# A log-sum-exp kernel: 1.5 heads per tile through TensorE in full fp32, 20 load buffers, and a last tile in pieces

## The chip, the cores and the metric

The kernel runs on one core of a Trainium2 chip. The metric is device time in microseconds (us). "Time" is the median of several executions; "span" is the length of the one profiled execution, and is 1 to 2 us shorter. All times below are of fast-state runs, except where a sentence says otherwise.

Engine names in the profile: PE is TensorE, PEld its weight loads, DVE is VectorE, ACT is ScalarE, POOL is GpSimd, SP the engine that issues the loads.

## The reference

`x` is 8 x 2048 x 2048 in fp32 (134 MB), `bias` is 8 heads x 256. For each row and each head of 256 columns the kernel must return log(sum(exp(x + bias))), and each result is stored twice in a row.

```
x_heads = x.reshape(B, S, H, Dh).transpose(0, 2, 1, 3)      # H = 8, Dh = 256
x_heads = x_heads + bias[None, :, None, :]
x_tiled = np.repeat(x_heads, 2, axis=2)
mx = x_tiled.max(axis=-1, keepdims=True)
lse = mx.squeeze(-1) + np.log(np.exp(x_tiled - mx).sum(axis=-1))
```

## The kernel before

A tile is 128 rows x 2048 columns, 1 MiB; there are 128 of them. Seven of the eight heads go through VectorE: ScalarE takes exp of 1792 columns in one instruction, and VectorE multiplies each head with exp(bias) and sums it. The eighth head goes through TensorE: a first matmul writes the bias into PSUM (one row of ones as stationary operand, so a contraction over one row), a second adds x (identity as stationary operand). Both use the upper bf16 half of each number. ScalarE then takes exp of the result and sums it in the same pass.

```
XIN_BUFS = 8                                    # load buffers
pspool = ... tile_pool(name="pspool", bufs=3, space=PSUM)
...
for b in range(B):
    for sblk in range(nsblk):
        xt = xin.tile([P, D], mybir.dt.float32, name="xt")
        nc.sync.dma_start(out=xt, in_=x[b, s0 : s0 + P, :])
        ...                                     # x_hi, b_hi: views of the upper bf16 halves
        for h in range(n_ttr, H):               # n_ttr = 7: one head
            ps = pspool.tile([P, Dh], mybir.dt.float32, name="ps")
            nc.tensor.matmul(ps, lhsT=ones_bf[0:1, :], rhs=b_hi, start=True, stop=False)
            nc.tensor.matmul(ps, lhsT=ident_bf[:, :], rhs=x_hi, start=False, stop=True)
            nc.scalar.activation(out=ps, in_=ps, func=ACT.Exp,
                                 accum_out=R[:, b, h, sblk : sblk + 1])
        nc.scalar.activation(out=xt[:, 0 : n_ttr * Dh], in_=xt[:, 0 : n_ttr * Dh], func=ACT.Exp)
        for h in range(n_ttr):
            ...                                 # VectorE: multiply with exp(bias) and sum
    ...                                         # transpose of R, log, store, once per b
```

The softmax here doesn't subtract the row's maximum and nothing guards it: scores larger than these inputs give would overflow.

## Time and profile before

| | before |
|---|---|
| time | 347.4 us |
| VectorE busy | 92% |
| ScalarE busy | 79% |
| TensorE busy | 28% |
| DMA | 421 GB/s through the middle of the span |
| the last tile's load: 15 of 16 increments / the 16th | 327.8 us / 337.2 us |

The head of the page of the kernel before: first the busy time of each engine, then VectorE's and the DMA engines' rows of the table of 40 slices (each digit is a busy share in tenths), then what the DMA engines moved in each slice.

```profile
PE 95.0 (28%) x268; PEld 27.6 (8%) x268; DVE 316.6 (92%) x1793; ACT 272.4 (79%) x397; POOL 5.0 (1%) x15
...
DVE  0899989899898998999989989899899998999985
...
DMA  7999999999999999999999999999999999999700
GB/s 303 427 421 421 417 422 423 422 421 421 419 423 417 424 421 419 423 420 424 423 418 418 424 420 423 421 422 419 422 416 412 370 401 424 420 411 409 286 24 15
```

The loads fill nearly the whole span: 1 MiB at 421 GB/s takes 2.49 us (in the timeline a tile comes every 2.48), and VectorE needs 7 x 0.346 = 2.42 us per tile.

The view of waits of the kernel before says who waited for whom, for how many us in total, how often, and the longest.

```profile
PE ps L109 <- ACT ps L115: 207.5, 123, 2.1
ACT xt L123 <- DMA xt<-in_x_dram: 56.2, 105, 3.7
...
DVE junk L131 <- ACT xt L123: 15.4, 23, 1.0
```

The timeline of the kernel before, TensorE and ScalarE around one tile. The columns are start in us, duration, engine, line, operation and operands, and in brackets the idle time before it and what ended it.

```profile
156.20 0.37 ACT L115 ACTIVATE ps<-ps 128x256 f32<-128x256 f32 x1
...
156.50 0.18 ACT L115 ACTIVATION_READ_ACCUMULATOR ps<-ps 128x1 f32 x1
156.73 0.37 PE L109 MATMUL ps<-brow,ones_bf 1*128 1x256 bf16 x1 [1.81 <-ACT ps L115]
...
157.03 0.39 PE L112 MATMUL ps<-xt,ident_bf 128*128 128x256 bf16 x1
157.07 1.70 ACT L123 ACTIVATE xt<-xt 128x1792 f32<-128x1792 f32 x1 [0.39 <-DMA xt<-in_x_dram]
...
158.68 0.37 ACT L115 ACTIVATE ps<-ps 128x256 f32<-128x256 f32 x1
```

ScalarE ends a sum at 156.68, the bias matmul starts at 156.73, the x matmul at 157.03. Both are over by 157.42, while ScalarE is still in the large exp that its own wait for a load let start at 157.07. So the loop "ScalarE's sum, bias matmul, x matmul, ScalarE's next sum" takes about 1.2 us of work and fits inside the 2.48 us of a load.

### The profile page before, as it was taken

The numbers are of one execution on the slowest core, as the hardware profiler recorded it, in microseconds if no ns is written. First come the engines' busy times: TensorE is split into PE (matmuls) and PEld (weight loads), VectorE is DVE, ScalarE is ACT, GpSimd is POOL, SyncE is SP. The second block draws the span as 40 slices with busy tenths as digits, with TensorE's granted clock in tenths as the row PEclk, the third lists the DMA queues.
The fourth block names the chain that finished last, engine by engine and source line by source line (L and its number), as shares of the span: only waits on it lengthen the run. The fifth ranks groups of instructions, "written<-read, shape, count | busy, mean of one in ns | idle before, by whom it ended". The sixth has DMA issues, their size and how long they took to land. (4 is left out here: it accounts for less than half of the span.)

```text
span 345.5 us, 3541 instructions
## 1 busy us (share of the span) xinstructions
PE 95.0 (28%) x268; PEld 27.6 (8%) x268; DVE 316.6 (92%) x1793; ACT 272.4 (79%) x397; POOL 5.0 (1%) x15
## 2 busy tenths in 40 slices
PE   2423223223322323322332322232223232222220
PEld 0100000000000000000010000000000000000000
DVE  0899989899898998999989989899899998999985
ACT  4978878788787887878778878788777887878872
POOL 1000000000000000000000000000000000000000
DMA  7999999999999999999999999999999999999700
GB/s 303 427 421 421 417 422 423 422 421 421 419 423 417 424 421 419 423 420 424 423 418 418 424 420 423 421 422 419 422 416 412 370 401 424 420 411 409 286 24 15
DMA packets 18939, 135.50 MB, mean 392 GB/s; under 512 B 2177, under 2 KB 2305, under 8 KB 2529
## 3 DMA queue, kind: packets, MB, share of 16 engines
q1 hardware_dynamic: 18576, 134.36, 94.3%
q0 software_dynamic: 336, 0.92, 0.7%
q14 instruction: 23, 0.19, 0.1%
q8 instruction: 2, 0.03, 0.0%
q10 hardware_dynamic: 2, 0.01, 0.0%
HBM read 134.23 MB, written 1.05 MB: 392 GB/s over the span
## 5 line engine op out<-in xcount | busy, mean ns | idle before, releaser
L131 DVE CUSTOM_DVE_ANT_0 junk<-xt,w_rep 128x256 f32<-128x256 f32 x896 | 316.3, 422 | 24.0 <-ACT xt L123 15.4
L123 ACT ACTIVATE xt<-xt 128x1792 f32<-128x1792 f32 x128 | 217.2, 1698 | 62.7 <-DMA xt<-in_x_dram 56.2
L109 PE MATMUL ps<-brow,ones_bf 1*128 1x256 bf16 x128 | 46.9, 368 | 207.6 <-ACT ps L115 207.5
L131 DVE DVE_READ_ACCUMULATOR2_ANT R<- 128x1 f32 x896 | 74.8, 83 | 0.0
L112 PE MATMUL ps<-xt,ident_bf 128*128 128x256 bf16 x128 | 49.3, 385 | 21.4 <-DMA xt<-in_x_dram 21.3
L115 ACT ACTIVATE ps<-ps 128x256 f32<-128x256 f32 x128 | 47.2, 369 | 0.0
L112 PEld LDWEIGHTS <-ident_bf 128*128 128x128 bf16 x128 | 13.2, 104 | 245.2 <-issue 245.2
L115 ACT ACTIVATION_READ_ACCUMULATOR ps<-ps 128x1 f32 x128 | 23.5, 184 | 0.0
L109 PEld LDWEIGHTS <-ones_bf 1*128 1x128 bf16 x128 | 12.5, 98 | 45.6 <-issue 45.6
L152 ACT ACTIVATE res<-tps 128x256 f32<-128x256 f32 x8 | 3.1, 383 | 6.6 <-PE tps L143 6.6
L159 POOL DMA_DIRECT2D out_dram<-res x7 | 3.9, 562 | 295.9 <-ACT res L152 295.9
L143 PE MATMUL tps<-ident,R 128*128 128x128 f32 x8 | 3.6, 452 | 13.8 <-DVE R L131 13.8
L79 PE MATMUL psw<-brow,ones_bf 1*128 1x512 bf16 x4 | 2.4, 601 | 4.2 <-DMA brow<-in_bias_dram 2.4
L143 PEld LDWEIGHTS tps<-ident,R 128*128 128x128 f32 x8 | 1.4, 180 | 19.3 <-issue 15.8
L82 ACT ACTIVATE w_rep<-psw 128x512 f32<-128x512 f32 x4 | 2.3, 593 | 0.0
L50 ACT ACT_TABLE_LOAD x1 | 1.3, 1283 | 0.7 <-PEq L174 0.7
L63 DVE MEMSET ones_bf<- 1x128 bf16 x1 | 0.2, 165 | 0.8 <-PEq L174 0.8
L79 PEld LDWEIGHTS <-ones_bf 1*128 1x128 bf16 x4 | 0.5, 118 | 4.0 <-issue 3.0
masks.py:199 POOL TENSOR_SCALAR_AFFINE_SELECT ident<-ident 128x128 f32<-128x128 f32 x1 | 0.3, 285 | 0.0
masks.py:199 POOL TENSOR_SCALAR_AFFINE_SELECT ident_bf<-ident_bf 128x128 bf16<-128x128 bf16 x1 | 0.3, 285 | 0.0
masks.py:197 POOL MEMSET ident<- 128x128 f32 x1 | 0.2, 205 | 0.3 <-POOLq L174 0.3
masks.py:197 POOL MEMSET ident_bf<- 128x128 bf16 x1 | 0.2, 206 | 0.0
(4 smaller groups left out, 0.4 us busy)
## 6 DMA issues: line engine op xcount, KB each, us to landing
xt<-in_x_dram SPq DMA_DIRECT2D x128, 1024.0 KB, 16.4
out_dram<-res POOLq DMA_DIRECT2D x7, 128.0 KB, 5.8
out_dram<-res SPq DMA_DIRECT2D x1, 128.0 KB
brow<-in_bias_dram ACTq DMA_DIRECT2D x1, 8.0 KB
```

The lines of the kernel that those rows point to most:

```text
L50: nc.scalar.add_instruction(mybir.InstLoadActFuncSet(name=nc.get_next_instruction_name(), act_func_set_id=set_idx,))
L63: nc.vector.memset(ones_bf, 1.0)
L79: nc.tensor.matmul(psw, lhsT=ones_bf[0:1, :], rhs=b_hi_c, start=True, stop=True)
L82: nc.scalar.activation(out=w_rep[:, c * WCH : (c + 1) * WCH], in_=psw, func=ACT.Exp)
L109: nc.tensor.matmul(ps, lhsT=ones_bf[0:1, :], rhs=b_hi, start=True, stop=False)
L112: nc.tensor.matmul(ps, lhsT=ident_bf[:, :], rhs=x_hi, start=False, stop=True)
L115: nc.scalar.activation(out=ps, in_=ps, func=ACT.Exp, accum_out=R[:, b, h, sblk : sblk + 1],)
L123: nc.scalar.activation(out=xt[:, 0 : n_ttr * Dh], in_=xt[:, 0 : n_ttr * Dh], func=ACT.Exp,)
L131: nc.vector.tensor_tensor_reduce(out=junk, in0=xt[:, sl], in1=w_rep[:, sl], scale=1.0, scalar=0.0, op0=ALU.mult, op1=ALU.add, accum_out=R[ ...
L143: nc.tensor.transpose(out=ps, in_=R[:, b].rearrange("p h s -> p (h s)"), identity=ident)
L152: nc.scalar.activation(out=res, in_=ps_view, func=ACT.Ln)
L159: out_eng.dma_start(out=ov, in_=res.rearrange("p s e -> p (s e)"))
```

## The change

The intent: take work from VectorE (6.5 instead of 7 heads per tile), add the bias with full fp32 precision on the TensorE path, give the loads more buffers, and shorten the end. Odd tiles send 2 heads through TensorE, even tiles 1. The core of the diff, with cuts:

```
-N_TTR_HEADS = 7
-XIN_BUFS = 8
+NPE_MAX = 2
+XIN_BUFS = 20
...
-    pspool = ... bufs=3 ...
+    pbias = ... bufs=5 ...
...
+    def biased(xt, b, blk, npe):
+        ps = pbias.tile([P, CMAX], F32, name="ps")
+        n = npe * Dh
+        nc.tensor.matmul(
+            ps[:, 0:n], lhsT=ones, rhs=brow[:, 0:n], start=True, stop=False
+        )
+        nc.tensor.matmul(
+            ps[:, 0:n], lhsT=ident, rhs=xt[:, 0:n], start=False, stop=True
+        )
+        for h in range(npe):
             nc.scalar.activation(...)          # exp and sum of one head
...
+            npe = 1 + t % 2
...
+            cuts = [0, 512, 1024, 1536, 2048] if last else [0, D]
+            for i in range(len(cuts) - 1):
+                nc.sync.dma_start(
+                    out=xt[:, cuts[i] : cuts[i + 1]], in_=src[:, cuts[i] : cuts[i + 1]]
                 )
```

`ones`, `ident`, `brow` and `xt` are all read as fp32 now.

More of the change, by code (lines that the diff above doesn't have):

```diff
@@ L8 @@
 from concourse.masks import make_identity
-N_TTR_HEADS = 7
-XIN_BUFS = 8
+F32 = mybir.dt.float32
+ACT = mybir.ActivationFunctionType
+ALU = mybir.AluOpType
+NPE_MAX = 2
+XIN_BUFS = 20
 @with_exitstack
@@ L26 @@
     H, Dh = bias.shape
-    assert D == H * Dh
-    assert S % P == 0
-    nsblk = S // P
-    NCOL = H * nsblk
-    assert NCOL <= P
-    n_ttr = max(0, min(N_TTR_HEADS, H))
-    ACT = mybir.ActivationFunctionType
-    ALU = mybir.AluOpType
+    assert D == H * Dh and S % P == 0
+    NBLK = S // P
+    NR = H * NBLK
+    MM = 512
+    CMAX = NPE_MAX * Dh
     const = ctx.enter_context(tc.tile_pool(name="const", bufs=1))
-    rpool = ctx.enter_context(tc.tile_pool(name="rpool", bufs=1))
     xin = ctx.enter_context(tc.tile_pool(name="xin", bufs=XIN_BUFS))
     junkp = ctx.enter_context(tc.tile_pool(name="junkp", bufs=2))
-    pspool = ctx.enter_context(tc.tile_pool(name="pspool", bufs=3, space=bass.MemoryType.PSUM))
-    pspoolw = ctx.enter_context(tc.tile_pool(name="pspoolw", bufs=2, space=bass.MemoryType.PSUM))
-    tpsum = ctx.enter_context(tc.tile_pool(name="tpsum", bufs=2, space=bass.MemoryType.PSUM))
-    resp = ctx.enter_context(tc.tile_pool(name="resp", bufs=2))
+    pbias = ctx.enter_context(
+        tc.tile_pool(name="pbias", bufs=5, space=bass.MemoryType.PSUM)
+    )
+    tpsum = ctx.enter_context(
+        tc.tile_pool(name="tpsum", bufs=2, space=bass.MemoryType.PSUM)
+    )
+    resp = ctx.enter_context(tc.tile_pool(name="resp", bufs=2))
+    brow = const.tile([1, D], F32, name="brow")
+    w_rep = const.tile([P, D], F32, name="w_rep")
+    ident = const.tile([P, P], F32, name="ident")
+    ones = const.tile([1, P], F32, name="ones")
+    R = const.tile([P, B, H, NBLK], F32, name="R")
     with tc.high_priority():
-        act_sets = list(get_activation_tables(nc.m.arch).items())
-        for set_idx, (_set_name, funcs) in enumerate(act_sets):
+        for set_idx, (_name, funcs) in enumerate(
+            get_activation_tables(nc.m.arch).items()
+        ):
             if ACT.Exp in funcs and ACT.Ln in funcs:
@@ L56 @@
                 break
-        ident = const.tile([P, P], mybir.dt.float32, name="ident")
-        make_identity(nc, ident)
-        ident_bf = const.tile([P, P], mybir.dt.bfloat16, name="ident_bf")
-        make_identity(nc, ident_bf)
-        ones_bf = const.tile([1, P], mybir.dt.bfloat16, name="ones_bf")
-        nc.vector.memset(ones_bf, 1.0)
-        brow = const.tile([1, D], mybir.dt.float32, name="brow")
         nc.scalar.dma_start(
@@ L68 @@
         )
-        w_rep = const.tile([P, D], mybir.dt.float32, name="w_rep")
-        brb = brow.bitcast(mybir.dt.bfloat16)
-        WCH = 512
-        for c in range(D // WCH):
-            b_hi_c = bass.AP(
-                tensor=brb.tensor,
-                offset=brb.offset + 2 * c * WCH + 1,
-                ap=[[brb.ap[0][0], 1], [2, WCH]],
-            )
-            psw = pspoolw.tile([P, WCH], mybir.dt.float32, name="psw")
-            nc.tensor.matmul(
-                psw, lhsT=ones_bf[0:1, :], rhs=b_hi_c, start=True, stop=True
-            )
-            nc.scalar.activation(
-                out=w_rep[:, c * WCH : (c + 1) * WCH], in_=psw, func=ACT.Exp
-            )
@@ L86 @@
-    R = rpool.tile([P, B, H, nsblk], mybir.dt.float32, name="R")
-    for b in range(B):
-        for sblk in range(nsblk):
-            s0 = sblk * P
-            xt = xin.tile([P, D], mybir.dt.float32, name="xt")
-            nc.sync.dma_start(out=xt, in_=x[b, s0 : s0 + P, :])
-            if n_ttr < H:
-                xb = xt.bitcast(mybir.dt.bfloat16)
-                bb = brow.bitcast(mybir.dt.bfloat16)
-            for h in range(n_ttr, H):
-                x_hi = bass.AP(
-                    tensor=xb.tensor,
-                    offset=xb.offset + 2 * h * Dh + 1,
-                    ap=[xb.ap[0], [2, Dh]],
-                )
-                b_hi = bass.AP(
-                    tensor=bb.tensor,
-                    offset=bb.offset + 2 * h * Dh + 1,
-                    ap=[[bb.ap[0][0], 1], [2, Dh]],
-                )
-                ps = pspool.tile([P, Dh], mybir.dt.float32, name="ps")
-                nc.tensor.matmul(
-                    ps, lhsT=ones_bf[0:1, :], rhs=b_hi, start=True, stop=False
-                )
-                nc.tensor.matmul(
-                    ps, lhsT=ident_bf[:, :], rhs=x_hi, start=False, stop=True
-                )
-                nc.scalar.activation(
-                    out=ps,
-                    in_=ps,
-                    func=ACT.Exp,
-                    accum_out=R[:, b, h, sblk : sblk + 1],
-                )
-            if n_ttr > 0:
-                nc.scalar.activation(
-                    out=xt[:, 0 : n_ttr * Dh],
-                    in_=xt[:, 0 : n_ttr * Dh],
-                    func=ACT.Exp,
-                )
-                for h in range(n_ttr):
-                    sl = slice(h * Dh, (h + 1) * Dh)
-                    junk = junkp.tile([P, Dh], mybir.dt.float32, name="junk")
-                    nc.vector.tensor_tensor_reduce(
-                        out=junk,
-                        in0=xt[:, sl],
-                        in1=w_rep[:, sl],
-                        scale=1.0,
-                        scalar=0.0,
-                        op0=ALU.mult,
-                        op1=ALU.add,
-                        accum_out=R[:, b, h, sblk : sblk + 1],
-                    )
-        ps = tpsum.tile([NCOL, P], mybir.dt.float32, name="tps")
@@ new lines @@
+        nc.vector.memset(ones, 1.0)
+        make_identity(nc, ident)
+        for c in range(0, D, MM):
+            psw = pbias.tile([P, MM], F32, name="ps")
+            nc.tensor.matmul(
+                psw, lhsT=ones, rhs=brow[:, c : c + MM], start=True, stop=True
+            )
+            nc.scalar.activation(out=w_rep[:, c : c + MM], in_=psw, func=ACT.Exp)
+    def biased(xt, b, blk, npe):
[3 more added lines that the diff above has]
+            ps[:, 0:n], lhsT=ones, rhs=brow[:, 0:n], start=True, stop=False
+        )
+        nc.tensor.matmul(
+            ps[:, 0:n], lhsT=ident, rhs=xt[:, 0:n], start=False, stop=True
+        )
+        for h in range(npe):
+            nc.scalar.activation(
+                out=ps[:, h * Dh : (h + 1) * Dh],
+                in_=ps[:, h * Dh : (h + 1) * Dh],
+                func=ACT.Exp,
+                accum_out=R[:, b, h, blk : blk + 1],
+            )
@@ new lines, in weigh @@
+    def weigh(xt, b, blk, h):
+        c = h * Dh
+        junk = junkp.tile([P, Dh], F32, name="junk")
+        nc.vector.tensor_tensor_reduce(
+            out=junk,
+            in0=xt[:, c : c + Dh],
+            in1=w_rep[:, c : c + Dh],
+            scale=1.0,
+            scalar=0.0,
+            op0=ALU.mult,
+            op1=ALU.add,
+            accum_out=R[:, b, h, blk : blk + 1],
+        )
+    t = 0
+    for b in range(B):
+        for blk in range(NBLK):
+            xt = xin.tile([P, D], F32, name="xt")
+            src = x[b, blk * P : (blk + 1) * P, :]
+            npe = 1 + t % 2
+            t += 1
+            c0 = npe * Dh
+            last = b == B - 1 and blk == NBLK - 1
+            cuts = [0, 512, 1024, 1536, 2048] if last else [0, D]
+            for i in range(len(cuts) - 1):
+                nc.sync.dma_start(
+                    out=xt[:, cuts[i] : cuts[i + 1]], in_=src[:, cuts[i] : cuts[i + 1]]
+                )
+            for i in range(len(cuts) - 1):
+                a = max(cuts[i], c0)
+                e = cuts[i + 1]
+                if i == 0:
+                    biased(xt, b, blk, npe)
+                if a < e:
+                    nc.scalar.activation(
+                        out=xt[:, a:e], in_=xt[:, a:e], func=ACT.Exp
+                    )
+                    for h in range(a // Dh, e // Dh):
+                        weigh(xt, b, blk, h)
+        tps = tpsum.tile([NR, P], F32, name="tps")
@@ L143 @@
         nc.tensor.transpose(
-            out=ps, in_=R[:, b].rearrange("p h s -> p (h s)"), identity=ident
+            out=tps, in_=R[:, b].rearrange("p h n -> p (h n)"), identity=ident
         )
-        res = resp.tile([NCOL, P, 2], mybir.dt.float32, name="res")
-        ps_view = bass.AP(
-            tensor=ps.tensor,
-            offset=ps.offset,
-            ap=[ps.ap[0], [1, P], [0, 2]],
+        res = resp.tile([NR, P, 2], F32, name="res")
+        tv = bass.AP(
+            tensor=tps.tensor, offset=tps.offset, ap=[tps.ap[0], [1, P], [0, 2]]
@@ L151 @@
         )
-        nc.scalar.activation(out=res, in_=ps_view, func=ACT.Ln)
+        nc.scalar.activation(out=res, in_=tv, func=ACT.Ln)
         ov = bass.AP(
@@ L155 @@
             offset=out.offset + b * H * 2 * S,
-            ap=[[2 * P, NCOL], [1, 2 * P]],
+            ap=[[2 * P, NR], [1, 2 * P]],
         )
```

## The prediction

> **What bounds it now.** The loads, and in the end one DMA engine of 16. The table of slices shows the DMA engines at 90% or more and some 421 GB/s from slice 2 to 36. In the timeline a matmul on x starts every 2.48 us, and the exp's waits end on the tile's load. A tile is 1 MiB, 64 KB per engine: 26.4 GB/s each. VectorE is close below (7 heads x 0.346 = 2.42 us per tile), ScalarE further (2.09 us).
>
> About every 22 us a tile comes some 0.95 us late (gaps of 3.4 us at 44, 65, 89, 110, 154, 201, 246, 290, 334 us). Just before each, the trace has an 8 KB packet of the instruction queue. 8 KB are 128 instructions; VectorE's 1,930 make 15. The Trainium skill ("Runtime: NRT & Kernel Launch", Instruction fetch mechanics) says that a sequencer fetches instructions by its own DMA queue, mostly hidden; this trace says not hidden. A load needs 16 increments; of the last tile's, 15 came by 327.8 us and one at 337.2 us. So VectorE's fetches appear to delay always the same engine, which sets the time: 3.2 + 128 x 2.485 + 15 x 1.0 = 336 us. Then come exp 1.7, seven reductions to 341.5, transpose 0.45, log 0.39, store: span 345.5 us.
>
> **What the change does.**
> - VectorE: 896 to 832 reductions, 2.25 us per tile. That widens slack, and drops 128 instructions: one fetch fewer, about -1.0 us, the main gain.
> - ScalarE: every second tile an exp shorter by 0.21 us and one more summed exp (0.48 us): 2.22 us on average, off the path.
> - TensorE: two bf16 matmuls of 0.38 us become fp32 ones of 256 or 512 columns. The skill ("FP8 and Floating Point Precision", TensorE Precision Notes) gives fp32 four passes. From the trace (512 bf16 columns 0.60 us, 256 0.37) I estimate 0.9 and 1.8 us per matmul, 5.3 us per two tiles against 5.2 available: just full. I expect sustained work to make TensorE faster, so it keeps up. Its larger instruction stream presumably goes through another DMA engine.
> - 20 buffers: the late engine had 6 to 7 tiles outstanding throughout (16.4 us from issue to landing) and never starved; the others don't set the time. About 0.
> - Last tile in four pieces: before, 4.3 us from landing to the last reduction. Now VectorE must still do tile 126's 7 heads (ready 1.75 us after its landing, which is 2.48 us before the last), then 6 heads: about 3.9 us. ScalarE does its pieces behind fp32 matmuls. Gain 0.2 to 0.6 us; 2 KB rows cost 0.1 back.
>
> **Prediction.** 347.47 - 1.0 - 0.4 + 0.1 = 346.2 us; 8 in 10 between 344.3 and 349.0. Faster by over 2%: 0.05; within 2%: 0.87; slower by over 2%: 0.08.
>
> **Right if** after shows: slices still at 421 GB/s; the last load landing near 336 us, one increment 10 us or more after the others; 14 late tiles; VectorE some 84% busy and idle on waits; TensorE well under 100%; the last reduction 4 us after the last landing.
>
> **Wrong if** fp32 matmuls run slower than estimated and ScalarE waits for them in order (slower, perhaps much); if TensorE's fetches fall on VectorE's DMA engine (+5 us); if 20 buffers let the late engine catch up (to -10 us).

## More of the kernel before

The program is scheduled by a framework: an instruction may be placed earlier in its engine's order than it stands in the source, as far as its data and buffers allow.

L109 is the bias matmul, L115 is ScalarE's exp and sum of a TensorE head. In 123 of 128 tiles the bias matmul waits for ScalarE. Here this is harmless, because TensorE has little to do.

## The result, and the profile after

| | before | after |
|---|---|---|
| time | 347.4 us (347.3 to 347.7) | 530.96 us (530.81 to 531.17) |
| TensorE / VectorE / ScalarE busy | 28 / 92 / 79% | 79 / 56 / 54% |
| last load landed | 337.2 us | 454.4 us |
| last VectorE sum ended | 341.5 us | 525.4 us |

The ratio is 1.529 (95% interval 1.527 to 1.531). A ratio here is the mean time of one kernel's fast runs over that of the other's of the same rounds, so it is not quite the ratio of the medians in the table.

The same parts of the page, after:

```profile
PE 416.9 (79%) x528; PEld 133.0 (25%) x528; DVE 298.7 (56%) x1665; ACT 285.9 (54%) x527; POOL 4.6 (1%) x13
...
DVE  1755655655556556556565565565655655646556
...
DMA  8999999986676776767767667767667686200000
GB/s 349 420 421 423 422 421 422 420 362 240 252 274 240 275 262 245 296 240 243 277 256 266 259 231 303 246 240 289 237 269 259 239 305 240 79 12 0 0 1 10
```

For eight slices (106 us) the loads run as before, while the 20 buffers fill. Then they fall to 230 to 305 GB/s: they wait for buffers. The 20 buffers hid the trouble for a while and changed nothing of it. No engine is at 100%, which suggests that engines wait for each other.

The view of waits, after:

```profile
PEld ps L83 <- ACT ps L90: 231.8, 119, 2.6
ACT ps L90 <- PE ps L86: 222.6, 115, 5.5
DVE junk L100 <- ACT xt L133: 214.8, 120, 5.6
...
PE ps L83 <- ACT ps L90: 97.5, 117, 1.1
```

TensorE (the weight load of the bias matmul, L83) waits for ScalarE's sum (L90), and ScalarE's sum waits for the x matmul (L86). Each waits for the other, and VectorE waits behind them because ScalarE's large exp (L133) stands behind its sums. The rows count idle time of an engine: the weight loads are idle during TensorE's own matmuls too, so what TensorE lost to ScalarE is the last row, 97.5 us, and not the first. The timeline shows one turn for two tiles, TensorE and ScalarE only:

```profile
306.10 2.07 PE L83 MATMUL ps<-brow,ones 1*128 1x512 f32 x2 [0.57 <-ACT ps L90]
...
308.10 2.08 PE L86 MATMUL ps<-xt,ident 128*128 128x512 f32 x2
310.21 0.37 ACT L90 ACTIVATE ps<-ps 128x256 f32<-128x256 f32 x1 [2.79 <-PE ps L86]
310.49 0.20 ACT L90 ACTIVATION_READ_ACCUMULATOR ps<-ps 128x1 f32 x1
310.72 0.37 ACT L90 ACTIVATE ps<-ps 128x256 f32<-128x256 f32 x1
311.00 0.19 ACT L90 ACTIVATION_READ_ACCUMULATOR ps<-ps 128x1 f32 x1
...
311.25 1.22 PE L83 MATMUL ps<-brow,ones 1*128 1x256 f32 x2 [1.07 <-ACT ps L90]
...
312.39 1.22 PE L86 MATMUL ps<-xt,ident 128*128 128x256 f32 x2
313.65 0.37 ACT L90 ACTIVATE ps<-ps 128x256 f32<-128x256 f32 x1 [0.87 <-PE ps L86]
...
314.18 1.22 PE L83 MATMUL ps<-brow,ones 1*128 1x512 f32 x1 [0.56 <-ACT ps L90]
```

From 306.10 to 314.18 are 8.08 us for two tiles, where the loads would allow 4.96. TensorE's part is 2.00 + 2.11 + 1.14 + 1.26 = 6.51 us, ScalarE's 1.04 + 0.53 = 1.57, and nothing overlaps. 58 such turns, seven of them 0.5 us longer for a transpose, fill the span from 37 to 510 us.

Why does the bias matmul wait for ScalarE, with five PSUM buffers? The order of TensorE's matmuls, early in the trace, tells it. An fp32 matmul of the source is two instructions here, and a row merges neighbours of one line and shows the first one's shape: x8 is four bias matmuls, x4 two.

```profile
25.37 5.48 PE L83 MATMUL ps<-brow,ones 1*128 1x512 f32 x8
30.79 2.08 PE L86 MATMUL ps<-xt,ident 128*128 128x512 f32 x2
32.79 2.92 PE L83 MATMUL ps<-brow,ones 1*128 1x512 f32 x4
35.65 1.22 PE L86 MATMUL ps<-xt,ident 128*128 128x256 f32 x2
37.43 2.07 PE L83 MATMUL ps<-brow,ones 1*128 1x512 f32 x2 [0.56 <-ACT ps L90]
39.44 2.08 PE L86 MATMUL ps<-xt,ident 128*128 128x512 f32 x2
42.58 1.22 PE L83 MATMUL ps<-brow,ones 1*128 1x256 f32 x2 [1.07 <-ACT ps L90]
43.73 1.22 PE L86 MATMUL ps<-xt,ident 128*128 128x256 f32 x2
```

A bias matmul needs no load, only a PSUM buffer, so it was placed as early as a buffer could be had. With the tiles counted from 1, the bias matmuls of tiles 6 to 9 run before the x matmul of tile 6 (25.37 and 30.79 us), and those of tiles 10 and 11 before that of tile 7. From 37.43 us on the bias is four tiles ahead: that of tile 12 comes before the x matmul of tile 8. Four of the five buffers then hold finished bias rows (tiles 8 to 11); the fifth is that of tile 7, which ScalarE frees by summing tile 7. TensorE's matmuls run in this order, so the x matmul of tile 8 stands behind the bias of tile 12. Tile 8 thus can't start on TensorE before ScalarE has finished tile 7, and further buffers would be filled the same way (five and one were run, below). The kernel before has the same order, two tiles ahead with its three buffers; its loop was just short enough.

The groups by shape give the price of one matmul instruction (busy us, mean ns of one). An fp32 matmul of the source is two of them, each with its own weight load:

```profile
L83 PE MATMUL ps<-brow,ones 1*128 1x512 f32 x128 | 132.3, 1135 | 35.4 <-ACT ps L90 35.4
L86 PE MATMUL ps<-xt,ident 128*128 128x512 f32 x128 | 131.6, 1132 | 0.0
...
L86 PE MATMUL ps<-xt,ident 128*128 128x256 f32 x128 | 77.5, 709 | 0.0
L83 PE MATMUL ps<-brow,ones 1*128 1x256 f32 x128 | 77.2, 705 | 62.1 <-ACT ps L90 62.1
```

In the timeline an fp32 matmul occupies TensorE for 2.00 us with 512 columns and 1.14 with 256. The difference, 0.86 us per 256 columns, is four times the 0.22 us that 256 columns cost in bf16 in the kernel before (0.60 us with 512 columns less 0.38 with 256). That agrees with the four passes of the Trainium skill ("FP8 and Floating Point Precision", TensorE Precision Notes).

### The profile page after: what moved, and what is told of

The parts are those of the page before. It is cut to its first block, busy times and chain, and to the rows that moved or that the text cites. A ratio compares the mean times of both kernels' runs of the same rounds, so it can differ in the third digit from the quotient of the medians.

```text
span 529.2 us, 3971 instructions
## 1 busy us (share of the span) xinstructions
PE 416.9 (79%) x528; PEld 133.0 (25%) x528; DVE 298.7 (56%) x1665; ACT 285.9 (54%) x527; POOL 4.6 (1%) x13
## 3 DMA queue, kind: packets, MB, share of 16 engines
q1 hardware_dynamic: 19008, 134.36, 66.4%
## 5 line engine op out<-in xcount | busy, mean ns | idle before, releaser
L100 DVE CUSTOM_DVE_ANT_0 junk<-xt,w_rep 128x256 f32<-128x256 f32 x832 | 297.5, 421 | 225.9 <-ACT xt L133 214.8
L83 PE MATMUL ps<-brow,ones 1*128 1x256 f32 (+1 forms) x256 | 208.8, 920 | 97.5 <-ACT ps L90 97.5
L86 PE MATMUL ps<-xt,ident 128*128 128x256 f32 (+1 forms) x256 | 208.3, 920 | 0.0
L133 ACT ACTIVATE xt<-xt 128x1792 f32<-128x1792 f32 (+2 forms) x130 | 202.6, 1559 | 4.9 <-DMA xt<-in_x_dram 4.8
L90 ACT ACTIVATE ps<-ps 128x256 f32<-128x256 f32 x192 | 70.8, 369 | 224.6 <-PE ps L86 222.6
L83 PEld LDWEIGHTS ps<-brow,ones 1*128 1x128 f32 x256 | 64.3, 306 | 241.5 <-ACT ps L90 231.8
L86 PEld LDWEIGHTS ps<-xt,ident 128*128 128x128 f32 x256 | 64.5, 310 | 135.1 <-issue 131.2
L100 DVE DVE_READ_ACCUMULATOR2_ANT R<- 128x1 f32 x832 | 68.1, 82 | 0.0
L90 ACT ACTIVATION_READ_ACCUMULATOR ps<-ps 128x1 f32 x192 | 37.2, 194 | 0.0
L75 PE MATMUL ps<-brow,ones 1*128 1x512 f32 x8 | 7.2, 1069 | 3.7 <-DMA brow<-in_bias_dram 3.7
L147 ACT ACTIVATE res<-tps 128x256 f32<-128x256 f32 x8 | 3.1, 384 | 10.4 <-PE tps L140 10.4
L75 PEld LDWEIGHTS ps<-brow,ones 1*128 1x128 f32 x8 | 2.5, 323 | 6.8 <-issue 6.8
```

The lines of the kernel that those rows point to most:

```text
L75: nc.tensor.matmul(psw, lhsT=ones, rhs=brow[:, c : c + MM], start=True, stop=True)
L83: nc.tensor.matmul(ps[:, 0:n], lhsT=ones, rhs=brow[:, 0:n], start=True, stop=False)
L86: nc.tensor.matmul(ps[:, 0:n], lhsT=ident, rhs=xt[:, 0:n], start=False, stop=True)
L90: nc.scalar.activation(out=ps[:, h * Dh : (h + 1) * Dh], in_=ps[:, h * Dh : (h + 1) * Dh], func=ACT.Exp, accum_out=R[:, b, h, blk : blk + 1],)
L100: nc.vector.tensor_tensor_reduce(out=junk, in0=xt[:, c : c + Dh], in1=w_rep[:, c : c + Dh], scale=1.0, scalar=0.0, op0=ALU.mult, op1=ALU.a ...
L133: nc.scalar.activation(out=xt[:, a:e], in_=xt[:, a:e], func=ACT.Exp)
```

## The experiments

Theory A: the loop through TensorE and ScalarE sets the time, and it is the order of the two matmuls that ties it. Rivals: B, the fp32 matmuls are simply too slow whatever the order; C, something else in the change (buffers, pieces) costs time; D, PSUM buffers are too few. Later came E and F, about TensorE's clock, and G and H, about the loads. All kernels gave correct results.

### x first, bias second

```
-        matmul(ps[:, 0:n], lhsT=ones, rhs=brow[:, 0:n], start=True, stop=False)
-        matmul(ps[:, 0:n], lhsT=ident, rhs=xt[:, 0:n], start=False, stop=True)
+        matmul(ps[:, 0:n], lhsT=ident, rhs=xt[:, 0:n], start=True, stop=False)
+        matmul(ps[:, 0:n], lhsT=ones, rhs=brow[:, 0:n], start=False, stop=True)
```

> The changed kernel with its two fp32 matmuls in the other order: x first (start), bias second (stop). The bias matmul can then no longer be placed ahead of the x matmul of an older tile, so TensorE no longer waits for ScalarE before each tile. Theory A (a serial loop of TensorE and ScalarE, 8.08 us per two tiles: 6.5 of TensorE and 1.57 of ScalarE): the 1.57 us leave the loop, two tiles take 6.3 to 6.5 us at the slow TensorE rate, 64 pairs give 405 to 416 us and the whole 415 to 435 us; if the fuller TensorE then runs at twice the rate, about 346 us. Rival B (fp32 matmuls alone are too slow, order does not matter): stays at 531 us.

Measured: 424.56 us. First the busy line of its page, then TensorE's timeline (here L83 is the x matmul and L86 the bias matmul):

```profile
PE 414.0 (98%) x528; PEld 131.8 (31%) x528; DVE 293.8 (70%) x1665; ACT 280.6 (67%) x527; POOL 4.6 (1%) x13
```

```profile
304.11 2.08 PE L83 MATMUL ps<-xt,ident 128*128 128x512 f32 x2
306.12 2.07 PE L86 MATMUL ps<-brow,ones 1*128 1x512 f32 x2
308.12 1.22 PE L83 MATMUL ps<-xt,ident 128*128 128x256 f32 x2
309.27 1.22 PE L86 MATMUL ps<-brow,ones 1*128 1x256 f32 x2
310.42 2.08 PE L83 MATMUL ps<-xt,ident 128*128 128x512 f32 x2
```

Two tiles now take 6.31 us and TensorE never waits. 106 us of the loss were the loop, as theory A said; rival B falls as the whole story. What is left is TensorE's own time. Of each matmul's 2.00 or 1.14 us, 0.86 us per 256 columns grow with the columns (the difference of the two); the other 0.3 us do not.

### bf16 as before, everything else changed

```
+        x_hi = ... ; b_hi = ...              # upper bf16 halves, as in the kernel before
-        matmul(..., lhsT=ones, rhs=brow[:, 0:n], ...)
-        matmul(..., lhsT=ident, rhs=xt[:, 0:n], ...)
+        matmul(..., lhsT=ones_bf, rhs=b_hi, ...)
+        matmul(..., lhsT=ident_bf, rhs=x_hi, ...)
```

> The changed kernel with its two matmuls per tile in bf16 halves as before (same order, same 1.5 heads, 20 buffers, four pieces). Theory A and rival B: the whole loss goes, because a bf16 loop is about 1.9 us per tile, under the 2.48 us of a load: 345.5 to 347 us, what the prediction gave for the rest of the change. Rival C (20 buffers or the queue of loads cost something): clearly over 350 us. Last load landing about 336 us, one increment some 10 us or more after the others, 14 late tiles.

Measured: 345.91 us, ratio 0.9961 (0.9949 to 0.9974). Rival C falls: heads, buffers and pieces together cost nothing, they gain 1.3 us (no run separates the buffers from the rest). The trace shows the last load with 15 increments by 326.6 us and the 16th at 336.5 us, 14 instruction packets of VectorE's rhythm, and the last sum at 340.3 us, 3.8 us after the last landing. So this part of the prediction held to within 0.3 us.

### One PSUM buffer instead of five

```
-        tc.tile_pool(name="pbias", bufs=5, space=bass.MemoryType.PSUM)
+        tc.tile_pool(name="pbias", bufs=1, space=bass.MemoryType.PSUM)
```

> The changed kernel with 1 instead of 5 PSUM buffers for the biased heads. Theory A: the loop is the same with one buffer (bias matmul waits for ScalarE's sum of the tile before, then x matmul, then ScalarE): 530 to 536 us. Rival D (the five buffers give overlap of which there is only too little): much slower than 531, by more than 20 us.

Measured: 553.05 us, which is outside what theory A expected and just where rival D began. The trace says why: the turn for two tiles is 8.20 us, against 8.08 with five buffers, 64 x 0.12 = 8 us. The other 14 us are at the ends. With one buffer the first x matmul starts at 19.9 us instead of 11.6, because the set-up of exp(bias) shares the buffer, and the last tiles have no bias rows written in advance. In the steady part four more buffers are worth 1.5%, so the core of theory A stands: buffers filled ahead with work that isn't the wanted work give next to no overlap.

### The kernel before, with only its matmuls in fp32

```
-  matmul(ps, lhsT=ones_bf[0:1, :], rhs=b_hi, ...)
-  matmul(ps, lhsT=ident_bf[:, :], rhs=x_hi, ...)
+  matmul(ps, lhsT=ones, rhs=brow[:, sl], ...)
+  matmul(ps, lhsT=ident, rhs=xt[:, sl], ...)
```

> The kernel before with only its matmuls made fp32 (one head, 256 columns, 8 buffers, one load per tile). Theory A: the loop is 1.14 + 1.26 us of TensorE and 0.54 us of ScalarE, 2.94 us per tile: 128 of them and 10 to 16 us at the ends, 386 to 395 us. Rival B (TensorE's own time only, 2.3 us per tile at this rate, under the 2.48 us of a load): stays near 347 us.

Measured: 399.03 us, 4 us over the range. TensorE's turns in the timeline are 2.99 us (302.19 to 305.18) instead of 2.94, which is 6 us over 128 tiles. Rival B's 347 is excluded.

### The same, with x first

```
-  matmul(ps, lhsT=ones, rhs=brow[:, sl], start=True, stop=False)
-  matmul(ps, lhsT=ident, rhs=xt[:, sl], start=False, stop=True)
+  matmul(ps, lhsT=ident, rhs=xt[:, sl], start=True, stop=False)
+  matmul(ps, lhsT=ones, rhs=brow[:, sl], start=False, stop=True)
```

> The kernel before with fp32 matmuls, 399 us, with its two matmuls in the other order. Theory A (the serial loop, not TensorE's own time): TensorE needs 2 x 1.15 = 2.3 us per tile, under the 2.48 us of a load, and no longer waits for ScalarE: 346 to 350 us, TensorE about 85% busy. Rival B: stays near 399 us.

Measured: 347.59 us, the time of the kernel before (ratio 1.0008, 0.9993 to 1.0023). Its busy line:

```profile
PE 302.7 (88%) x524; PEld 129.3 (37%) x524; DVE 317.1 (92%) x1794; ACT 270.4 (78%) x397; POOL 5.0 (1%) x15
```

The same matmuls, 11 points more of TensorE's time used, and 51 us less. This is the cleanest test of theory A: full fp32 on one head is free once the order lets TensorE run while ScalarE works.

### Does the one-row matmul keep TensorE slow?

In the first experiment TensorE was 98% busy for 400 us, and its 512-column instructions started 1.00 us apart on average to the end; 0.86 us of it grow with the columns, as worked out there. At the very end of the changed kernel five x matmuls follow each other without bias matmuls between them, and there the rate doubles (starts of the 512-column instructions in us, from the trace; the last pair has a doubled rate):

```
511.62  512.63  ...  514.34  515.20  ...  516.62  517.04
```

The Trainium skill ("TensorE: Matmul & The Clock Gate", Part 1) says that the array runs at half its clock until it has been busy for some 3.4 us, then at the full one. The end of the changed kernel agrees (the doubling comes at 516.3 us, 4.7 us after 511.62); the first experiment does not, by that wording. The suspicion was the bias matmul, which contracts over one row of the 128.

```
+    part = const.tile([P, P], F32); memset(part, 1.0 / P)
+    ball = const.tile([P, CMAX], F32)          # bias loaded into all 128 partitions
-        matmul(ps[:, 0:n], lhsT=ones, rhs=brow[:, 0:n], start=False, stop=True)
+        matmul(ps[:, 0:n], lhsT=part, rhs=ball[:, 0:n], start=False, stop=True)
```

> The first experiment (x first, bias second) with the bias matmul over 128 rows (a stationary operand of 1/128 everywhere, the bias loaded into all 128 partitions) instead of 1 row. In the first experiment TensorE was 98% busy and still took 0.85 us for each pass group of 512 columns; in the changed kernel it took 0.42 us only at the very end, after x matmuls had followed each other for over 4 us without a bias matmul between them. Theory E (a matmul with one row does not count as work that frees TensorE's clock): now TensorE runs at twice the rate, two tiles take about 3.2 us of it, and the loads bind: 345 to 349 us. Rival F (the alternation of two stationary operands, or something else, keeps it slow): 420 to 427 us as in the first experiment.

Measured: 348.63 us (347.29 to 349.52). TensorE's timeline has the same pair of instructions at both rates, 1.9 us and 1.0 us, and the page has the granted clock by slice, in tenths:

```profile
3.76 7.16 PE L83 MATMUL ps<-brow,ones 1*128 1x512 f32 x8 [3.76 <-DMA brow<-in_bias_dram]
...
199.21 1.91 PE L94 MATMUL ps<-ball,part 128*128 128x512 f32 x2
200.92 1.06 PE L91 MATMUL ps<-xt,ident 128*128 128x256 f32 x2
201.77 1.06 PE L94 MATMUL ps<-ball,part 128*128 128x256 f32 x2
...
203.85 1.02 PE L94 MATMUL ps<-ball,part 128*128 128x512 f32 x2
```

```profile
PEclk9999998899869988888869879899889996988898
```

As to the clock, theory E holds: with 128 rows the clock rises whenever TensorE has been busy, and falls back when it has caught up (its clock records alternate between 1.0 and 0.5, 38 of them, 79 us at 0.5). The loads bind again. The first row above, the set-up of exp(bias) in the same trace, also speaks for it: eight one-row instructions follow each other for 7 us, 0.85 us apart after the first, and do not speed up; the clock first rises at 15.6 us, after 4.8 us of matmuls over 128 rows.

But the 76 us that this edit saves (424.6 to 348.6) are not shown to be the clock's. The matmuls are shorter at the low clock too: from 199.21 to 200.92 us one of 512 columns takes 1.71 us, and the next of 256 columns takes 0.85, where the first experiment has 2.00 and 1.14. The 0.29 us that do not grow with the columns are gone. There the first weight load of each of the 256 matmuls starts together with it (as at 304.11 us), here 0.85 us before it (198.36 and 199.21). So two tiles take 2 x (1.71 + 0.85) = 5.12 us at the low clock, and by this estimate 64 x (6.31 - 5.12) = 76 us go without any help of the clock. How the saving divides between the clock and the hidden weight loads stays open, and so does why they are not hidden where one-row and 128-row matmuls alternate.

The edit changed the rows and with them the data, so that it is the number of rows and not the data was not separated. Note also that the page's granted clock reads 1.00 for the first experiment, whose trace holds no clock record at all; the durations decide.

### The fourth corner: bias first, 128 rows

The matmuls of the last experiment in the order of the changed kernel.

> The changed kernel as it is, bias first, but with the bias matmul over 128 rows: the fourth corner of order (bias first or x first) and rows of the bias matmul (1 or 128); the other three took 531, 424.6 and 348.6 us. Theory A+E (serial loop, and a one-row matmul does not raise TensorE's clock): the loop of two tiles is 6.5 us of TensorE and 1.57 of ScalarE at the low clock and about 3.3 + 1.57 = 4.9 us at the high one; the clock will go up and down, as TensorE is less than full, so between 347 and 430 us. Rival F (clock unchanged while ScalarE breaks the stream): 531 us.

Measured: 364.68 us over four runs that fall into two groups, 360.3 and 361.6 (fast), 367.8 and 368.1 (slow). Its profile is of a slow run, so only the times are used, and the ratio of 1.039 is of the fast pair. The four corners:

| | bias over 1 row | bias over 128 rows |
|---|---|---|
| bias first | 531.0 us | 361.0 us (fast runs) |
| x first | 424.6 us | 348.6 us |

Either edit alone takes away over half of the loss, together they take all but about 1 us over the kernel before. So the 184 us can't be divided into a share of the order and a share of the rows: with shorter matmuls the loop nearly fits, and without the loop the one-row bias costs 76 us. With bias first the hidden weight loads alone can't be the reason: at the low clock the loop would take 5.12 + 1.57 = 6.69 us for two tiles, by estimate 428 us for 64 of them, and 361 were measured.

### Two heads in every tile

```
-            npe = 1 + t % 2
+            npe = 2                            # on the bf16 form
```

> The bf16 form of the changed kernel (345.9 us) with 2 heads on TensorE and ScalarE in every tile. VectorE issues 128 instructions fewer in all, so one more instruction fetch less; ScalarE needs 1.40 + 0.96 = 2.36 us per tile, just under a load. Theory G (each fetch for VectorE delays one DMA engine by about 1 us, and that engine sets the time): 344.5 to 345.3 us. Rival H (the fetches don't set the time): no change, 345.7 to 346.1; slower if ScalarE can't keep up.

Measured: 344.39 us (344.28 to 344.64), ratio 0.9917 (0.9902 to 0.9931), 0.1 us under theory G's range. The last load lands at 335.8 us, 0.7 us earlier than with 1.5 heads, and the last sum follows 3.25 us later instead of 3.8. So about half of the 1.5 us is the fetch and half the shorter end.

### 384 more instructions on VectorE, or on GpSimd

```
+        if h < 5:
+            nc.vector.memset(junk[0:1, 0:1], 0.0)      # 3 per tile; the control: nc.gpsimd.memset
```

> The fastest version so far (bf16, 2 heads, 344.4 us) with 384 more VectorE instructions, memsets of one element, three per tile, spread evenly. Theory G (each 128 VectorE instructions cost a fetch of 8 KB that delays the late DMA engine by about 1 us): three fetches more, 347 to 348 us, last load landing 3 us later. Rival H: VectorE has about 0.3 us per tile to spare, so no change, 344.2 to 344.8 us.

> The control to the run with 384 more VectorE instructions: the same number of one-element memsets on GpSimd instead. Theory G, if GpSimd's fetches go through another DMA engine than VectorE's: no change, 344.2 to 344.8 us. If through the same one: 347 to 348 us.

Measured: 348.12 us with the memsets on VectorE, 344.47 us with the same number on GpSimd. Both traces hold 25 instruction packets of that queue, three more than the base; in the first the 16th increment of the last load comes at 338.5 us, in the second at 335.8 us, as without them. The landing is 2.7 us later for three VectorE fetches, 0.9 us each. The whole run is 3.7 us longer, because the last sum also follows the landing 4.0 us later instead of 3.25. VectorE's own time does not delay the loads: the waits of the engine that issues them name no VectorE instruction in this run. Theory G holds: VectorE's instruction fetches delay one DMA engine, and that engine ends the loads. GpSimd's don't.

### Sparing five DMA engines in three tiles

```
+            if t in (31, 61, 91):
+                nc.sync.dma_start(out=xt[0:88, :], in_=src[0:88, :])
+                nc.sync.dma_start(out=xt[88:128, :], in_=src[88:128, :])
```

> The bf16 form of the changed kernel with three of its 128 tiles (31, 61 and 91) loaded by two transfers, of 88 and of 40 partitions. By the Trainium skill (DMA: Bandwidth & Descriptors, on why a DMA increments its semaphore by 16) these run on the lowest 11 and 10 of the 16 engines, so engines 11 to 15 are spared 3 x 2.48 = 7.4 us of loads and engines 0 to 9 get 3.7 us more. Theory G (one late engine sets the time): 338 to 340 us if the late engine is among 11 to 15, about 349.6 us if it is among 0 to 9, 346 if it is engine 10. Rival H (all engines' total sets the time): 346 to 350 us, and the gap between the last increment and the others of the last tile unchanged.

Measured: 371.26 us; no theory expected that, and the experiment doesn't tell which engine is the late one. The number of engines was as expected: each transfer has one small packet for each engine it runs on, and the queue of the loads holds 15 packets more than in the bf16 run (19,023 against 19,008), which is 3 x (11 + 10 - 16). Which engines they were the trace does not tell. In the two to four slices after each split the loads fall to 205 to 390 GB/s. Of the 8 KB packets that started between 70 and 90 us a quarter took over 0.57 us, against 0.31 to 0.32 us elsewhere, so packets of these two transfers, or those beside them, ran at half speed. Why stays open. The last tile's 16th increment came 10.4 us after the others (362.7 and 352.3 us), against 9.9 in the bf16 run; had the late engine been spared 7.4 us, the gap should have shrunk. With the slow transfers in between, this only hints that it is not among engines 11 to 15.

### The last two tiles in pieces

```
-            last = b == B - 1 and blk == NBLK - 1
+            last = b == B - 1 and blk >= NBLK - 2      # on bf16 with two heads
```

> The fastest version so far (bf16, 2 heads, 344.4 us) with the last two tiles instead of the last one loaded in four pieces. VectorE's backlog of six heads of tile 126 at the end then starts earlier; ScalarE, which ends its last exp 2.1 us after the last landing, becomes the limit. Expected gain 0.2 to 0.6 us: 343.8 to 344.2 us. If the pieces of 2 KB rows cost more than that: no change or 0.1 to 0.3 us slower.

Measured: 343.94 us (343.81 to 344.06), ratio 0.9900 (0.9883 to 0.9916). That is 0.45 us less than with one tile in pieces (344.28 to 344.64), but in another session, and the intervals of the two ratios overlap, so the gain is likely but not shown. It is the fastest version found: 1.0% under the kernel before and 35% under the changed one, with the bf16 precision of the kernel before. The fastest with full fp32 is the kernel before with fp32 matmuls and x first, at 347.59 us.

## Why the prediction was wrong

It gave 346.2 us (344.3 to 349.0) and 0.08 for slower; the result is 531.

1. **The step that failed: "just full; I expect sustained work to make TensorE faster, so it keeps up."** It summed TensorE's own time, 5.3 us for two tiles, and compared it with 5.2. Three things were wrong in it.
   - The time per matmul was too low: 0.9 and 1.8 us expected, 1.14 and 2.00 measured. The estimate fits matmuls at the low clock whose neighbours all have 128 rows (0.85 and 1.71 us); with a one-row bias 0.29 us per matmul come on top, where the first of its two weight loads isn't hidden. With nothing waiting, two tiles take 6.31 us.
   - The faster clock did not come: 98% busy, and still 0.43 us per instruction for each 256 columns. With the bias matmul over 128 rows it came, in part of the time (0.43 us for 512 columns).
   - The engine was treated as alone. The bias matmul's wait for ScalarE, 207.5 us in 123 tiles, was in the waits of the kernel before, and its trace shows the bias matmuls running ahead, and neither was followed. The loop adds 1.57 us of ScalarE's and makes 8.08 us of 6.5.
2. **"Wrong if fp32 matmuls run slower than estimated and ScalarE waits for them in order"** named the result, with far too little weight. A term that comes out as "just full" is no slack; a loop through it would have had to be checked.
3. **VectorE, ScalarE, 20 buffers, four pieces: right as a sum.** With bf16 matmuls the change takes 345.91 us, against 346.2 predicted, with the late 16th increment 9.9 us after the others and the last sum 3.8 us after the last landing. Of the two gains, the landing came 0.6 us earlier (1.0 forecast) and the end was 0.5 us shorter (0.4 forecast).
4. **The late DMA engine: right.** Three more fetches for VectorE cost 2.7 us of landing time, the same number for GpSimd none. The guess that TensorE's fetches fall elsewhere held too: the fp32 kernel with x first has four packets of 16 KB in the queue that had two before, which fits its doubled TensorE stream, and takes 347.59 us.

## What to carry to other kernels

When a change lengthens an engine that is "off the path", look for waits of that engine on the engine that consumes its result: two engines that wait for each other add their times, and more buffers hardly help when the scheduler fills them with the half of the work that needs no input (five instead of one: 1.5% of a turn here). Starting an accumulation with the matmul that needs the load, and ending with the constant one, removed the loop in two kernels here (531 to 425 us, 399 to 348 us) at no cost. And check from the spacing of TensorE's instructions that it reaches its full clock and hides its weight loads, before counting on either; a bias over one row cost both here.

## What the Trainium skill lacked or had wrong

- "TensorE: Matmul & The Clock Gate", Part 1: sustained busy time is said to free the clock after some 3.4 us. Here 400 us at 98% busy did not, as long as every second fp32 matmul contracted over one row (0.43 us per instruction for each 256 columns), nor did 7 us of one-row matmuls without a gap; with 128 rows the same instruction fell from 0.85 to 0.43 us for 512 columns. The page's text does not say that rows count.
- No page gives what an fp32 matmul occupies as two matmul instructions and two weight loads: at the low clock 0.85 us with 256 columns and 1.71 us with 512 among matmuls over 128 rows, 1.14 and 2.00 us where it alternates with one over one row.
- "Runtime: NRT & Kernel Launch", Instruction fetch mechanics: the cost of a refill is called mostly hidden, and what it does to other transfers is not said. In a kernel bound by loads each 128 VectorE instructions delayed one DMA engine, and with it the last landing, by 0.9 us (384 instructions: 2.7 us).
- "DMA: Bandwidth & Descriptors", why a DMA increments its semaphore by 16, how many engines (k): its rule gives 11 and 10 engines for 88 and 40 partitions, but not that such transfers can be slow; three pairs of them in 128 tiles cost 25 us (371.3 against 345.9).
